# Opening of a two-layer FNet/attention kernel: modulation rows turned by transposes and summed on DVE, held weights' casts, earlier first weights

## Chip, cores and metric

One core of one Trainium2 chip runs the whole program. The metric is the device time of one execution in microseconds; the number given for a kernel is the median of its timed runs. A profile is one more execution, taken by the hardware profiler; its span runs from the first to the last instruction.

## What is computed

Two residual layers on 256 tokens of width 2048, with 256 context tokens beside them (512 columns in all). Layer 0 is a Fourier mixer, layer 1 a windowed attention with a prefix. Every layer first normalises its input and modulates it with a shift, a scale and a gate that a vector `c` gives through a 2048 x 6144 matrix. Cut to the part that the change touches:

```python
for i in range(DEPTH):                      # 2 layers
    shift, scale, gate = split(silu(c) @ ada_w[i] + ada_b[i], 3)
    h = rmsnorm(x, norm_g[i]) * (1 + scale) + shift
    # the same for the context, with c_ctx
    if kind == 0:
        u, z = split(h @ w_in, 2)           # 2048 -> 2 x 4096
        f = real(fft2(u, over tokens and over 256 channels of each of 16 groups))
        y = einsum('bngc,gcd->bngd', f, w_mix) * silu(z)
    ...
    x = x + gate * (y @ w_out[i])
return rmsnorm(x, final_g)
```

## The kernel before

Everything is float32; a product is made as three passes on TensorE (PE): each operand is cast to a rounded half `h` (on ScalarE, ACT) and the difference `l` is made on VectorE (DVE); `split` does this pair and `mm3` the passes h*h, h*l and l*h. The layouts of the weights in memory are prepared so that each load is one tile of 128 partitions by 2048 floats, 1 MB.

The change lies in the opening, which makes three things at once:

- The DFT over tokens of the normalised input. `x_split` splits the input in four blocks `nb` of 512 features, `dft_unit(k)` makes the DFT of one of 16 feature tiles k (128 features each), `evac_dft` copies it out of PSUM, and `scale_hx(k)` later multiplies it by its scale and splits it.
- The modulation rows of layer 0, as 32 strips of the matrix `awp`, 1 MB each. `ada_tile(i)` (L191) loads strip i with `raw_st` and multiplies it with the two modulation vectors (each of the four products counts as two matmuls in the profile, L197). Four strips, two steps, make one bank of PSUM for four feature tiles: scale (`which` = 1) or shift (0). The four products of a strip go to four 32-partition blocks, two rows of each in use, so the bank holds partial sums in four blocks. `ada_rows` (L199) copies the bank to `rows` on ACT (L201). `ada_fin` (L204) turns the rows into columns and sums the four blocks in one go, by four matmuls with `rows` as weights and a 128 x 2 selector `sel` (L207), and adds the bias on DVE (L210, L212) to give `gs0` or `sh0`.
- The first weights: halves kh = 0 and 1 of groups g = 0 and 1 of `wu`, tiles (g, kh). `load_uh` loads one, `fold_uh` (L122) makes a difference `wm` (L124) and a sum (L126) of its two parts on DVE, `split_uh` (L132) splits both into four tiles.

`opening_step(p)` (L269), p from 0 to 15, runs two strips and the work between them; at odd p the row copy follows. Steps over 7 have no DFT unit left and take units of `fill` by `fill_pe` (L372), three matmuls each, from the products of groups 0 and 1 with the 16 scaled tiles: there are 80 units, 56 of them in the steps and 24 behind the last. `fix_f0(nb)` sets column 0 of four scaled tiles from the shift, so a product that reads column 0 (parts `p` and `s`) waits for the shift and one of part `m` doesn't.

Strips and first weights share five slots of 1 MB: three of the pool `raw` (loads at L46) and two of the opening alone (L185). `raw_st` takes the slot whose number `until` is lowest; a strip has its own step there, a first weight the second argument. All these loads are issued by SyncE (SP), whose queue is in order: a load waits until the last reader of its slot is done, and those behind it wait too. Small loads go by ACT's queue, some by GpSimd's (POOL), which also issues a loading sum in later groups (L129).

Behind the opening the loop over 16 groups follows. `load_m(g)` (L323) prepares the mixing matrix, `part` makes the products of a group (parts m and p), `mix` multiplies with the mixing matrix (L463). `asp` (L440, L441 on ACT, L443 on DVE) holds the products of part `s`, and the first `mix` reads it.

Which order the instructions have on each engine is not the order of the text alone: the framework schedules them by its own estimate of when each can start. `tc.issue_after(ins)` binds that: what the block issues on the engine of `ins` comes behind `ins` on it.

Of the kernel before, what the change touches and what calls it, by code (L numbers as in the profile page):

```python
# [28 lines left out]
def tile_dit(ctx: ExitStack, tc: tile.TileContext, a: dict, out: bass.AP):  # L29
# [42 lines left out]
    def mm3(o, wh, wl, xh, xl, start, stop):  # L72
        PE.matmul(o, wh, xh, start=start, stop=False)  # L73
        PE.matmul(o, wh, xl, start=False, stop=False)  # L74
        PE.matmul(o, wl, xh, start=False, stop=stop)  # L75

    def rsqrt(pool, src, w, tag):
        v = pool.tile([P, w], F32, tag=tag + "v", name=tag + "v")
# [37 lines left out]
    sel = const.tile([P, 2], F32, name="sel")  # L116
    V.tensor_reduce(sel, ident.rearrange("p (c s) -> p s c", s=32)[:, 0:2, :], axis=AX.X, op=ALU.add)
# [23 lines left out]
    def load_u(g, after=None):  # L141
        v = [load_uh(g, kh) for kh in range(2)]
        with tc.issue_after(after) if after else nullcontext():
            return [split_uh(*fold_uh(v[kh], g, kh)) for kh in range(2)]

    lay0 = ctx.enter_context(ExitStack())
    adap = lay0.enter_context(tc.tile_pool(name="ada", bufs=1))
# [8 lines left out]
    with tc.tile_pool(name="st", reuse_waits="tile", bufs=1, side="right") as st:  # L156
# [29 lines left out]
            return t  # L186

        oa = [None]
        f0_end = [None]

        def ada_tile(i):  # L191
            nb, which, kg = i // 8, 1 - i // 4 % 2, i % 4
            t = raw_st(a["awp"][which, nb, kg], i // 2)
            if kg == 0:
                oa[0] = psum()
            for j in range(4):
                PE.matmul(oa[0][j * 32 : (j + 1) * 32, :], c32[:, kg * 4 + j, :], t[:, j * 512 : (j + 1) * 512], start=kg == 0, stop=kg == 3)  # L197

        def ada_rows():  # L199
            rows = st.tile([P, 512], F32, tag="rows", name="rows")  # L200
            S.copy(rows, oa[0])  # L201
            return rows

        def ada_fin(nb, which, rows):  # L204
            o2 = psum()
            for j in range(4):
                PE.matmul(o2[:, j * 2 : (j + 1) * 2], rows[:, j * P : (j + 1) * P], sel, start=True, stop=True)  # L207
# [31 lines left out]
        def dft_unit(k, ss_=(0, 1)):  # L239
            nb, j = k // 4, k % 4  # L240
            if k not in od:
                od[k] = psum()
            q = slice(j * P, (j + 1) * P)
            for s in ss_:
                for tt in range(2):
                    t = s * 2 + tt
                    h, l = xs[nb, t]
                    mm3(od[k][:, s * N : (s + 1) * N], h[:, q], l[:, q], dh[:, t, :], dl[:, t, :], tt == 0, tt == 1)

        def evac_dft(k):  # L250
            o = od.pop(k)
            r = act()
            S.copy(r, o)
            V.tensor_copy(f0[:, k, :], o[:, 0::N])
            hx.append(r)
# [10 lines left out]
        raws = {}  # L266
        units = {1: (), 2: (4, 5), 3: (6, 7), 4: (8, 9), 5: (10, 11), 6: (12, 13), 7: (14, 15)}

        def opening_step(p):  # L269
            nb, which = p // 4, 1 - p // 2 % 2  # L270
            if p == 0:
                x_split(0)
                for k in range(4):
                    dft_unit(k, (0,))
            for i in (2 * p, 2 * p + 1):
                ada_tile(i)
            if p in uload:
                raws[uload[p]] = load_uh(*uload[p], raw_st, {0: 7, 1: 12}[uload[p][1]])
            if p % 2:
                rows = ada_rows()  # L280
            if p == 1:
                for k in range(4):
                    dft_unit(k, (1,))
                    if k == 1:
                        ada_fin(nb, which, rows)
                for k in range(4):
                    evac_dft(k)
            else:
                for n, k in enumerate(units.get(p, ())):
                    dft_unit(k)  # L290
                    evac_dft(k)
                    if n == 0 and p % 2:
                        ada_fin(nb, which, rows)
                if p > 7:
                    fill_pe(4)
                    if p % 2:
                        ada_fin(nb, which, rows)
                    fill_pe(3)
# [52 lines left out]
        def u_step(g, nm, k):  # L351
            c0, c1 = dict(m=(128, 256), p=(0, 130))[nm]
            if k == 0:
                ou[g][nm] = psum()[0:127, 0 : 2 * (c1 - c0)].rearrange("p (s j) -> p s j", s=2)
            wh, wl = wu[g][k // 8][nm]
            h, l = hx[k]
            mm3(ou[g][nm], wh[:, k % 8, :], wl[:, k % 8, :], h[:, :, c0:c1], l[:, :, c0:c1], k == 0, k == KT - 1)

        def sp_step(k):
            if k == 0:  # L360
                ou[0]["s"] = psum()[0:32, 0:260].rearrange("p (s j) -> p s j", s=2)
            h, l = hx[k]
            q = slice(k * 32, (k + 1) * 32)
            mm3(ou[0]["s"], sph[:, q], spl[:, q], h[:, :, 0:130], l[:, :, 0:130], k == 0, k == KT - 1)
# [7 lines left out]
        def fill_pe(n):  # L372
            for _ in range(n):
                g, nm, k = fill.pop(0)
                sp_step(k) if nm == "s" else u_step(g, nm, k)

        for p in range(8, 16):
            if p == 8:
                wu[1][0] = split_uh(*raws[1, 0])
# [25 lines left out]
    ft_end = [None, None]  # L405
    asp = up.tile([96, 2, 130], F32R, name="asp", bufs=1)
    for g in range(G):
        w = load_u(g, f0_end[0] if g == 2 else None) if g > 1 else wu[g]
        if g == 0:
            am = []  # L410
            for i in range(2):
# [26 lines left out]
        if g == 0:  # L438
            ov = ou[0]["s"]
            S.copy(asp[0:32], ov)  # L440
            S.copy(asp[64:96], ov)  # L441
            pqh, pql, sp = m0
            V.tensor_tensor(asp[32:64], ov, asp[0:32].bitcast(F32), op=ALU.subtract)  # L443
# [726 lines left out]
```

## Time and profile before

| | us |
|---|---|
| median of 3 runs | 1876.44 (1874.44 to 1877.57) |
| the profiled execution | 1873.82 |
| its span | 1871.9 |
| PE busy in the span | 1826.4 (98%) |
| DVE busy | 1388.7 (74%) |
| ACT busy | 953.9 (51%) |
| mean granted clock of PE | 0.992 |

The profile's page gives busy time by engine, a picture of the span in 40 slices, the DMA queues, the chain of work that ended last, and the costliest groups of instructions. In the chain PE has 88% of the span. Other views of the same trace give the instructions of one engine in order of time, with the idle time before each and what ended it, and the busy time of every engine in a stretch. Times in them count from the span's start. The opening lasts to about 136 us; the strips' matmuls run from 17.37 to 120 us, and the eight row copies from 26.88 to 120.67 us.

### The profile page before, as it was taken

To read this page: it belongs to the slowest core of one execution; us is meant where nothing else is said; L and a number is where in the kernel's file an instruction comes from. 1 tells how busy PE (TensorE), PEld (TensorE's weight loads), DVE (VectorE), ACT (ScalarE), POOL (GpSimd) and SP (SyncE) were. 2 spreads that over 40 slices of the span, in tenths; PEclk is the share of its full clock that TensorE was granted. 3 is DMA by queue.
4 is the path that set the end of the run, shared out by engine and by line. 5 is a ranking of instruction groups with operands and counts; after the bars stand their busy time and mean duration, and the time that the engine had idled before them with its cause. 6 is when DMAs were issued, how large, how long until landed. Compare 5 with 4: busy or idle time off the path is not lost.

```text
span 1871.9 us, 26517 instructions
## 1 busy us (share of the span) xinstructions
PE 1826.4 (98%) x9921; PEld 1556.5 (83%) x9921; DVE 1388.7 (74%) x2760; ACT 953.9 (51%) x1661; POOL 175.3 (9%) x188
## 2 busy tenths in 40 slices
PE   6889999999999999999999999999999999999997
PEld 4669999888888888888888787888888888887886
DVE  4558888787768788687984835788778878887455
ACT  4435444432222243224221524888888888896343
POOL 0002111200000000000000001102221220300001
PEclk9999999999999999999999999999999999999999
DMA  9988888756666647763576323333333333434553
GB/s 395 352 299 235 227 224 233 253 219 230 236 230 222 228 163 259 281 224 135 224 268 224 131 90 135 136 128 120 125 124 135 116 132 134 159 135 171 189 180 135
DMA packets 75089, 366.89 MB, mean 196 GB/s; under 512 B 22161, under 2 KB 22305, under 8 KB 39889
## 3 DMA queue, kind: packets, MB, share of 16 engines
q1 hardware_dynamic: 49104, 324.83, 47.5%
q0 software_dynamic: 21280, 32.63, 6.8%
q10 hardware_dynamic: 4576, 7.74, 1.3%
q8 instruction: 78, 1.28, 0.3%
q14 instruction: 51, 0.41, 0.1%
HBM read 352.58 MB, written 12.59 MB: 195 GB/s over the span
## 4 chain that ended last, share of the span: by engine, by line
PE 88%; DVE 4%; DMA 3%; issue 2%; ACT 2%; POOL 0%; SPq 0%; POOLq 0%; ACTq 0%; DVEq 0%
PE ps L73 22%; PE ps L74 22%; PE ps L75 22%; PE ps L869 6%; PE ps L871 3%; PE ps L925 3%; DMA raw<-in_wu 2%; PE ps L940 2%; PE ps L939 2%; PE ps L905 1%; PE ps L906 1%; PE ps L197 1%; DMA raw<-in_awp 1%; DVE wpl L61 1%; ACT wh L60 0%
## 5 line engine op out<-in xcount | busy, mean ns | idle before, releaser
L60 ACT CAST wh<-raw 128x1024 fp32r<-128x1024 f32 x333 | 349.4, 1051 | 560.4 <-PE ps L74 496.1
L61 DVE TENSOR_TENSOR wl<-raw,wh 128x1024 fp32r<-128x1024 f32 x333 | 421.2, 1267 | 262.7 <-ACT wh L60 259.8
L74 PE MATMUL ps<-act,wh 128*128 128x512 f32 x1024 | 398.3, 389 | 0.0
L73 PE MATMUL ps<-act,wh 128*128 128x512 f32 x1024 | 393.7, 389 | 0.0
L75 PE MATMUL ps<-act,wl 128*128 128x512 f32 x1024 | 391.3, 389 | 0.0
L75 PEld LDWEIGHTS ps<-act,wl 128*128 128x128 f32 x1024 | 192.2, 188 | 39.9
L74 PEld LDWEIGHTS ps<-act,wh 128*128 128x128 f32 x1024 | 192.2, 188 | 39.8
L73 PEld LDWEIGHTS ps<-act,wh 128*128 128x128 f32 x1024 | 192.2, 188 | 39.8
L869 PE MATMUL ps<-h,wh 128*128 128x512 f32 x512 | 187.0, 400 | 0.0
L504 DVE CUSTOM_DVE_ANT_0 raw<-raw,cb 128x512 f32<-128x512 f32 x256 | 172.4, 687 | 18.8 <-DMA raw<-in_adw 15.0
L871 PE MATMUL ps<-h,wl 128*128 128x256 f32 x512 | 138.2, 280 | 0.0
L504 DVE CUSTOM_DVE_ANT_0 junk<-raw,cb 128x512 f32<-128x512 f32 x192 | 131.6, 685 | 6.7 <-ACT cb L496 5.6
L74 PE MATMUL ps<-wl,h 128*128 128x512 f32 x320 | 125.8, 393 | 1.5 <-DVE wl L61 1.5
L73 PE MATMUL ps<-wh,h 128*128 128x512 f32 x320 | 124.5, 397 | 0.2 <-ACT h L688 0.2
L75 PE MATMUL ps<-wh,h 128*128 128x512 f32 x320 | 124.5, 391 | 0.0
L869 PEld LDWEIGHTS ps<-h,wh 128*128 128x128 f32 x512 | 96.2, 188 | 19.0
L907 DVE CUSTOM_DVE_ANT_0 ps<-ps,mask,nsink 128x512 f32<-128x512 f32 x128 | 92.1, 753 | 12.3 <-PE ps L906 11.4
L910 ACT ACTIVATE p<-ps,mx 128x512 f32<-128x512 f32 x128 | 87.2, 686 | 24.7 <-DVE mx L907 24.1
L871 PEld LDWEIGHTS ps<-h,wl 128*128 128x128 f32 x512 | 96.8, 189 | 1.4
L61 DVE TENSOR_TENSOR pl<-ps,ph 128x512 fp32r<-128x512 f32 x128 | 83.6, 684 | 10.0 <-ACT ph L60 8.8
L915 ACT ACTIVATE p<-p,sm 128x512 f32<-128x512 f32 x128 | 85.5, 717 | 7.8 <-DVE sm L913 7.8
L74 PE MATMUL ps<-wl,ys 128*128 128x512 f32 x212 | 83.3, 393 | 0.0
(307 smaller groups left out, 3579.7 us busy)
## 6 DMA issues: line engine op xcount, KB each, us to landing
raw<-in_wz SPq DMA_DIRECT2D x64, 1024.0 KB, 4.9
raw<-in_adw SPq DMA_DIRECT2D x64, 1024.0 KB, 4.9
raw<-in_awp SPq DMA_DIRECT2D x32, 1024.0 KB, 8.6
raw<-in_wo SPq DMA_DIRECT2D x32, 1024.0 KB, 5.6
raw<-in_wq SPq DMA_DIRECT2D x32, 1024.0 KB, 4.8
raw<-in_wu SPq DMA_DIRECT2D x32, 1016.0 KB, 7.2
raw<-in_wo1b SPq DMA_DIRECT2D x16, 1024.0 KB, 4.8
act<-in_xT POOLq DMA_DIRECT2D x32, 256.0 KB, 5.2
```

Of the source, the lines that this page charges most:

```text
L60: S.copy(h, src)
L61: V.tensor_tensor(l, src, h.bitcast(F32), op=ALU.subtract)
L73: PE.matmul(o, wh, xh, start=start, stop=False)
L74: PE.matmul(o, wh, xl, start=False, stop=False)
L75: PE.matmul(o, wl, xh, start=False, stop=stop)
L504: V.tensor_tensor_reduce(junk if s == 0 and i < 3 else wf, wf, cb[:, s, kq * 512 : kq * 512 + 512], 1.0, 0.0, ALU.mult, ALU.add, acc[:, i, ...
L869: PE.matmul(o[0], wh[:, q], hx1[k], start=k == 0, stop=k == KT - 1)
L871: PE.matmul(o[0][:, 0:N], wl[:, q], hx1[k][:, 0:N], start=False, stop=False)
L907: V.tensor_tensor_reduce(o, o, mask[:, tb, :], -0.125, nsink[:, i : i + 1], ALU.add, ALU.min, mx[:, tb : tb + 1])
L910: S.activation(pt[:, tb, :], so[tb], AF.Exp, bias=mx[:, tb : tb + 1], scale=-1.0, accum_out=sm[:, tb : tb + 1])
L915: S.activation(pt[:, tb, :], pt[:, tb, :], AF.Copy, scale=sm[:, tb : tb + 1])
L925: PE.transpose(o[:, (kt * 2 + tb) * P : (kt * 2 + tb + 1) * P], pt[:, tb, c : c + P], ident)
```

## The change

- `ada_fin` is given an instruction `behind`. It makes four transposes of `rows` (128 x 128 each, a whole bank) instead of four matmuls with `sel`, puts them behind that instruction on PE, and sums the four blocks on DVE with one reduction of 128 x 32 elements to 128 x 8. `sel` and its reduction are gone.
- The turn of a step's rows is kept in `pend` and made after the first strip of the next step, with that strip's last matmul as `behind`; the last one comes after four units of the fill.
- In a step the first DFT unit, or three units of the fill, now stand ahead of the two strips, the rest behind them.
- The first weights (0, 0) and (1, 0) are loaded at steps 4 and 5 instead of 5 and 6; their `until` is 6 and 7 instead of 7, that of (0, 1) 11 instead of 12.
- The splits of all four first weights are issued behind the latest row copy at that place: those of steps 5, 7, 11 and 13.
- In group 2 the second half's fold and split, and `load_m(2)`, are issued behind the last instruction of `asp`. For groups over 2 both halves are loaded and folded before the first is split.

```diff
-        def ada_fin(nb, which, rows):
+        def ada_fin(nb, which, rows, behind):
             o2 = psum()
-            for j in range(4):
-                PE.matmul(o2[:, j * 2 : (j + 1) * 2], rows[:, j * P : (j + 1) * P], sel, start=True, stop=True)
+            with tc.issue_after(behind):
+                for j in range(4):
+                    PE.transpose(o2[:, j * P : (j + 1) * P], rows[:, j * P : (j + 1) * P], ident)
             kq = slice(nb * 4, nb * 4 + 4)
             dst = (sh0, gs0)[which][:, kq, :]
-            V.tensor_tensor(dst, o2[:, 0:8].rearrange("p (a b) -> p a b", b=2), adab[:, 0, which, kq], op=ALU.add)
+            V.tensor_reduce(dst, o2.rearrange("p (a j s) -> p a s j", a=4, j=4)[:, :, 0:2, :], axis=AX.X, op=ALU.add)
+            V.tensor_tensor(dst, dst, adab[:, 0, which, kq], op=ALU.add)
...
+            us_ = units.get(p, ())
+            if us_:
+                dft_unit(us_[0])
+                evac_dft(us_[0])
+            elif p > 7:
+                fill_pe(3)
             for i in (2 * p, 2 * p + 1):
-                ada_tile(i)
+                r = ada_tile(i)
+                if pend:
+                    ada_fin(*pend.pop(), r)
             if p in uload:
-                raws[uload[p]] = load_uh(*uload[p], raw_st, {0: 7, 1: 12}[uload[p][1]])
+                raws[uload[p]] = load_uh(*uload[p], raw_st, uhold[uload[p]])
             if p % 2:
-                rows = ada_rows()
+                pend.append((nb, which, ada_rows()))
...
-        uload = {5: (0, 0), 6: (1, 0), 9: (0, 1), 10: (1, 1)}
+        uload = {4: (0, 0), 5: (1, 0), 9: (0, 1), 10: (1, 1)}
+        uhold = {(0, 0): 6, (1, 0): 7, (0, 1): 11, (1, 1): 12}
...
-        opening_step(6)
         wu = [[None, None], [None, None]]
         raws[0, 0] = fold_uh(raws[0, 0], 0, 0)
+        opening_step(6)
+        with tc.issue_after(rows_end[0]):
+            wu[0][0] = split_uh(*raws[0, 0])
+        raws[1, 0] = fold_uh(raws[1, 0], 1, 0)
         opening_step(7)
-        wu[0][0] = split_uh(*raws[0, 0])
-        raws[1, 0] = fold_uh(raws[1, 0], 1, 0)
+        with tc.issue_after(rows_end[0]):
+            wu[1][0] = split_uh(*raws[1, 0])
...
                 if p == q + 1:
-                    wu[kh][1] = split_uh(*raws[kh, 1])
+                    with tc.issue_after(rows_end[0]):
+                        wu[kh][1] = split_uh(*raws[kh, 1])
+        while fill[0][2] < 12:
+            fill_pe(1)
+        r = fill_pe(4)
+        ada_fin(*pend.pop(), r)
         fix_f0(3)
         fill_pe(len(fill))
...
+        if g == 2:
+            v = [load_uh(g, kh) for kh in range(2)]
+            w = []
+            for kh in range(2):
+                with tc.issue_after((f0_end[0], asp_end)[kh]):
+                    w.append(split_uh(*fold_uh(v[kh], g, kh)))
...
-            with tc.issue_after(f0_end[0]) if g == 1 else nullcontext():
+            with tc.issue_after((f0_end[0], asp_end)[g - 1]) if g < 3 else nullcontext():
                 pqh, pql, sp = load_m(g)
```

More of the change, by code (lines that the diff above doesn't have):

```diff
@@ L74, in mm3 @@
         PE.matmul(o, wh, xl, start=False, stop=False)
-        PE.matmul(o, wl, xh, start=False, stop=stop)
+        return PE.matmul(o, wl, xh, start=False, stop=stop).ins
     def rsqrt(pool, src, w, tag):
@@ L115, in tile_dit @@
     V.tensor_copy(c32[:, :, 0:2], cc)
-    sel = const.tile([P, 2], F32, name="sel")
-    V.tensor_reduce(sel, ident.rearrange("p (c s) -> p s c", s=32)[:, 0:2, :], axis=AX.X, op=ALU.add)
     def load_uh(g, kh, ld=raw, *until):
@@ L139, in split_uh, with load_u @@
         return fl
[L141 to L144, printed above, removed]
+    def load_u(g):
+        return [split_uh(*f) for f in [fold_uh(load_uh(g, kh), g, kh) for kh in range(2)]]
     lay0 = ctx.enter_context(ExitStack())
@@ L188, in tile_dit @@
         oa = [None]
+        rows_end = [None]
         f0_end = [None]
@@ L196, in ada_tile @@
             for j in range(4):
-                PE.matmul(oa[0][j * 32 : (j + 1) * 32, :], c32[:, kg * 4 + j, :], t[:, j * 512 : (j + 1) * 512], start=kg == 0, stop=kg == 3)
+                r = PE.matmul(oa[0][j * 32 : (j + 1) * 32, :], c32[:, kg * 4 + j, :], t[:, j * 512 : (j + 1) * 512], start=kg == 0, stop=kg == 3)
+            return r.ins
         def ada_rows():
             rows = st.tile([P, 512], F32, tag="rows", name="rows")
-            S.copy(rows, oa[0])
+            rows_end[0] = S.copy(rows, oa[0]).ins
             return rows
-        def ada_fin(nb, which, rows):
+        def ada_fin(nb, which, rows, behind):
             o2 = psum()
-            for j in range(4):
-                PE.matmul(o2[:, j * 2 : (j + 1) * 2], rows[:, j * P : (j + 1) * P], sel, start=True, stop=True)
+            with tc.issue_after(behind):
+                for j in range(4):
+                    PE.transpose(o2[:, j * P : (j + 1) * P], rows[:, j * P : (j + 1) * P], ident)
             kq = slice(nb * 4, nb * 4 + 4)
             dst = (sh0, gs0)[which][:, kq, :]
-            V.tensor_tensor(dst, o2[:, 0:8].rearrange("p (a b) -> p a b", b=2), adab[:, 0, which, kq], op=ALU.add)
+            V.tensor_reduce(dst, o2.rearrange("p (a j s) -> p a s j", a=4, j=4)[:, :, 0:2, :], axis=AX.X, op=ALU.add)
+            V.tensor_tensor(dst, dst, adab[:, 0, which, kq], op=ALU.add)
             if which:
@@ L247, in dft_unit @@
                     h, l = xs[nb, t]
-                    mm3(od[k][:, s * N : (s + 1) * N], h[:, q], l[:, q], dh[:, t, :], dl[:, t, :], tt == 0, tt == 1)
+                    r = mm3(od[k][:, s * N : (s + 1) * N], h[:, q], l[:, q], dh[:, t, :], dl[:, t, :], tt == 0, tt == 1)
+            return r
         def evac_dft(k):
@@ L264, in scale_hx @@
             hx[k] = (h.rearrange("p (s j) -> p s j", s=2), l.rearrange("p (s j) -> p s j", s=2))
-        raws = {}
+        raws, pend = {}, []
         units = {1: (), 2: (4, 5), 3: (6, 7), 4: (8, 9), 5: (10, 11), 6: (12, 13), 7: (14, 15)}
@@ L283, in opening_step @@
                     dft_unit(k, (1,))
-                    if k == 1:
-                        ada_fin(nb, which, rows)
                 for k in range(4):
                     evac_dft(k)
[L288 to L298, printed above, removed]
+            elif us_:
+                dft_unit(us_[1])
+                evac_dft(us_[1])
+            elif p > 7:
+                fill_pe(4)
             if p in (1, 3, 5):
@@ L356, in u_step @@
             h, l = hx[k]
-            mm3(ou[g][nm], wh[:, k % 8, :], wl[:, k % 8, :], h[:, :, c0:c1], l[:, :, c0:c1], k == 0, k == KT - 1)
+            return mm3(ou[g][nm], wh[:, k % 8, :], wl[:, k % 8, :], h[:, :, c0:c1], l[:, :, c0:c1], k == 0, k == KT - 1)
         def sp_step(k):
@@ L363, in sp_step @@
             q = slice(k * 32, (k + 1) * 32)
-            mm3(ou[0]["s"], sph[:, q], spl[:, q], h[:, :, 0:130], l[:, :, 0:130], k == 0, k == KT - 1)
+            return mm3(ou[0]["s"], sph[:, q], spl[:, q], h[:, :, 0:130], l[:, :, 0:130], k == 0, k == KT - 1)
         fill = [(g, nm, k) for g in range(2) for nm in ("m", "p") for k in range(8)]
@@ L374, in fill_pe @@
                 g, nm, k = fill.pop(0)
-                sp_step(k) if nm == "s" else u_step(g, nm, k)
+                r = sp_step(k) if nm == "s" else u_step(g, nm, k)
+            return r
         for p in range(8, 16):
             if p == 8:
-                wu[1][0] = split_uh(*raws[1, 0])
                 cst = ua.tile([P, 4, P], F32, name="cst", bufs=1)
@@ L407, in tile_dit @@
     for g in range(G):
-        w = load_u(g, f0_end[0] if g == 2 else None) if g > 1 else wu[g]
+        if g == 2:
[4 more added lines that the diff above has]
+                    w.append(split_uh(*fold_uh(v[kh], g, kh)))
+        else:
+            w = load_u(g) if g > 1 else wu[g]
         if g == 0:
@@ L442, in tile_dit @@
             pqh, pql, sp = m0
-            V.tensor_tensor(asp[32:64], ov, asp[0:32].bitcast(F32), op=ALU.subtract)
+            asp_end = V.tensor_tensor(asp[32:64], ov, asp[0:32].bitcast(F32), op=ALU.subtract).ins
         mh, ml = am[g % 2]
```

## The prediction

> **What bounds the kernel now.** I read the table of busy shares first: PE 1826.4 us of a span of 1871.9, so all that can be had without removing PE work is 45 us. Then the table of stretches, to see where they lie.
>
> ```profile
> 30.00:40.00 10.00, 10.00 (x67) 5.50 (x60) 2.77 (x8) 4.06 (x10) 0.00 (x0) 0.85 1.01 414
> 60.00:70.00 10.00, 6.63 (x45) 4.99 (x45) 9.36 (x25) 7.18 (x15) 0.00 (x0) 0.85 1.02 425
> 70.00:80.00 10.00, 10.00 (x67) 7.13 (x65) 3.01 (x11) 1.21 (x2) 0.00 (x0) 0.81 0.88 325
> 80.00:90.00 10.00, 8.72 (x69) 4.87 (x68) 5.19 (x9) 5.31 (x10) 0.00 (x0) 1.00 0.83 323
> 130.00:140.00 10.00, 7.17 (x39) 6.95 (x38) 9.84 (x13) 3.59 (x6) 0.00 (x0) 0.66 0.81 181
> 150.00:160.00 10.00, 10.00 (x87) 10.00 (x85) 9.17 (x14) 5.27 (x10) 2.58 (x3) 1.00 0.89 283
> ```
>
> Columns: stretch, length, busy PE, PEld, DVE, ACT, POOL, granted clock, DMA share, GB/s. From 150 us PE makes 87 matmuls in 10 us, one per 0.115 us: its full rate, and it keeps it to 343 us but for some 2.7 us of gaps. So a microsecond won before 140 us should reach the end. Up to 60 us the transfers are full (413 to 424 GB/s, a 1 MB strip tile each 2.5 us; 352 in the last ten). From 50 to 120 us the stretches show 352, 425, 325, 323, 368, 416, 355 GB/s; against 420 they lack 376 x 10 us / 420 = 9.0 us. That is the most by which the last strip can come sooner. The third view is PE's timeline, first around 66 us, then at the end of the opening.
>
> ```profile
> 66.87 1.71 PE L207 MATMUL ps<-sel,rows 128*128 128x2 f32 x8 [3.37 <-ACT rows L201]
> 71.28 1.94 PE L197 MATMUL ps<-raw,c 128*32 128x512 f32 x8
> 76.77 1.06 PE L197 MATMUL ps<-raw,c 128*32 128x512 f32 x8
> ```
>
> ```profile
> 112.05 1.07 PE L197 MATMUL ps<-raw,c 128*32 128x512 f32 x8
> ...
> 113.87 1.05 PE L207 MATMUL ps<-sel,rows 128*128 128x2 f32 x8 [0.52 <-ACT rows L201]
> 114.86 2.78 PE L197 MATMUL ps<-raw,c 128*32 128x512 f32 x24
> ...
> 123.53 0.39 PE L73 MATMUL ps<-act,wph 128*127 128x260 f32 x1 [0.86 <-DVE act L221]
> ...
> 133.05 0.58 PE L463 MATMUL ps<-asp,sp 96*128 96x260 f32 x1 [2.83 <-DVE asp L443]
> ```
>
> In brackets stands PE's idle time and who ended it. L207 is the old turn of the modulation rows; it waits for the row copy L201. After the 3.37 us the same strip (8 matmuls, L197) takes 1.94 instead of 1.06 us: PE restarts at half rate, and the clock column shows 0.81. ACT's timeline says why that copy was late:
>
> ```profile
> 63.23 1.02 ACT L60 CAST wph<-raw 128x1016 fp32r<-128x1016 f32 x1
> 64.17 1.70 ACT L262 ACTIVATE act<-act,gs 128x256 fp32r<-128x256 f32 x4
> 65.77 0.56 ACT L253 COPY act<-ps 128x512 f32<-128x512 f32 x1
> 66.23 0.58 ACT L201 COPY rows<-ps 128x512 f32<-128x512 f32 x1
> ```
>
> Strip 15 ended at 63.5 us; the copy started at 66.23, behind a weights' cast and scalings.
>
> **Turn and sum (gain).** Before strip 15 the transfers set the pace, so I count nothing there. Behind it, PE waits for row copies 3.37 + 0.76 + 0.76 + 0.52 us (at 66.87, 83.69, 100.39, 113.87) and 0.86 at 123.53 for what follows the last: 6.3 us. With the turn behind the next strip (1.0 us of PE against 0.83 us from strip end to copied row) these go, if that strip has landed; if not, the turn and, behind it on PE, the second strip and the fill wait with it. The half rate after 66.87 goes with its wait: turn 1.57 us where 0.95 is usual, twelve matmuls 2.84 for 1.45, strip 1.86 for 1.00: 2.9 us. A turn of eight passes takes 0.91 to 0.98 us; the nearest row to four transposes is this one, 0.11 us each, so 0.44 us:
>
> ```profile
> 1041.59 2.78 PE L633 MATMUL ps<-ident,act 128*128 128x128 f32 x24
> ```
>
> Five turns by 0.5 us: 2.5. Together A = 11.7 us; bounds 9.0 (the transfers' slack) and 11.7. [...] DVE gains a reduction of 128x32 to 128x8 from PSUM, which no row shows: between 0.16 (a 128x8 reduction) and 0.69 (a 128x512 pass from PSUM), I take 0.2, the near row; eight of them, 1.6 us, lie in DVE's idle time (100 to 110 us: 1.16 busy of 10); without that cover only the last counts, 0.2. The removed sum into sel (0.17) was hidden.
>
> **Order behind asp (gain).** The last source of the wait at 133.05 is DVE's order:
>
> ```profile
> 128.87 0.42 DVE L329 TENSOR_TENSOR mt<-m 128x256 f32<-128x256 f32 x1
> 129.21 0.42 DVE L330 TENSOR_TENSOR mt<-m 128x256 f32<-128x256 f32 x1
> ...
> 132.57 0.42 DVE L443 TENSOR_TENSOR asp<-ps,asp 32x260 fp32r<-32x260 f32 x1
> ```
>
> asp's ACT inputs end at 128.36. The change puts group 2's second fold (1.17) and its load_m sums (0.67) behind it: 1.8 of the 2.83 us surely go. The remaining 1 us is of the size after which the rows show no slow phase (0.76, 0.86), so also the half rate goes: from 133.43, 12 matmuls at 0.215 and 18 in 3.35 us against 0.12 each, 2.3 us. B = 4.1; bounds 1.8 (half rate stays) and 5.1. What is pushed back, that fold's sums, is wanted some 5.8 us after asp (first mix 1.7, load_m 1.2, eight k of the first part 2.9) and needs about 3.5 (fold, cast, difference), so nothing for it.
>
> **Held casts (loss).** The edge puts each cast behind a row copy in ACT's order, so what ACT has queued behind the cast (scalings, evacuations) and DVE behind its difference waits for a strip too; ACT is busy only 3 to 7 of 10 there, so I price the slot: a first-weights tile keeps its slot of the five until its last difference. By the slot rule strip 28 takes the slot of the tile (1,1), whose casts now stand behind the row copy of step 13, that is behind strip 27. Before, its cast ran at 95.81, 17 us ahead of that copy. From strip 27's end: row copied 0.83, two casts 1.88 (63.23 to 64.17 is one), difference 1.21, the load at its shortest 4.8 (the shortest strip load in the trace is 4.7): 8.7 us, where it was 1.8. Behind strip 28 wait the scale rows of the last four k and all they feed; strips 29 to 31 have other slots. PE can fill with steps 14 and 15, 14 units of 0.36 us: 5.1. Idle 3.6, and a restart like that at 66.87, 2.9: C = 6.5; bounds 0 (more fill is left for it) and 11.6 (none). [...]
>
> **First weights sooner (loss).** The tile (0,0) was landed at 45.6 and not folded before 54.91, since x's strips hold the buffers; loading it a step sooner wins nothing and keeps a slot longer. On SP each of the two loads passes two strips: 10 to 13 land one transfer (2.5 us) later, 14 as before, and PE has the DFT units for that. Strip 15 now takes that slot, freed at 61.3 by the old times, where it was issued at 56.4; strip 18 takes (1,0)'s, held behind strip 15's row copy. SP's queue is in order, but strips 16 and 17 have free slots and can be ordered ahead. D between 0 and 4.9; I take 2.
>
> **The rest.** For groups over 2 both folds now come before both splits. Their data come some 4.5 us apart, and a split also waits for its buffers; I take 0, with -2.7 (the loop's gaps go) and +14.7 (13 groups by one fold of 1.13 us ahead of a split that PE awaits) as ends. Handing back instructions costs nothing.
>
> **Sum:** 11.7 + 4.1 - 6.5 - 2 = 7.3 us less. The profiled run took 1873.8 us with a span of 1871.9, so a span of about 1864.6; against the median of the runs shown, 1876.44 (2.6 over the profiled one), 1869.1.
>
> **Rivals.** (1) The holds starve the strips, and it is slower: C at its upper end 11.6, D at 4.9, and strip 27 behind tile (0,1): 8.7 less three transfers of 2.5 leaves 1.2, with a restart of 2.9, 4.1. 20.6 - 15.8 = +4.8, 1881. For it: with two weights held only three slots stream, and the median strip load is 8.6 us. Against: the fill. It decides where the last row copy, at 120.08 now, comes after some 124.2, where B no longer pays for it. (2) The gain stops at DVE: it has hardly a gap from 123.89 to 150, so PE can be ahead of it only by the slack at group 2. If strip 28 holds the last shift rows, DVE's block starts about 2 us sooner and the end moves by as little: 1874. For it: 9.84 of 10 busy; against: part of that block is what is pushed behind asp. (3) The holds cost nothing: 9.0 + 5.1 = 14.1, 1862. For it: the fill has 24 units more; against: eight of these need strip 27's rows, whose turn now stands behind strip 28. (4) The folds' order costs the loop half its upper end, 7.4 us, and the gain is gone: 1876. For it: PE waited for apl at 261.4 and 277.0 already.
>
> **Chances.** Forecast 0.42 (own range 1865 to 1873), rival 1 0.24, rival 2 0.14, rival 3 0.16, rival 4 0.04. A measurement here tells about 0.2%, 3.8 us, from no change. Faster: forecast and rival 3, 0.58. Same: rivals 2 and 4, 0.18. Slower: 0.24. The range takes in rival 3's value and rival 1's: 1861 to 1882.
>
> **What would show it.** A: no idle before the transposes, about 0.11 us each, and no clock of 0.81 around 70 us. B: the gap before L463 at most 1 us and a clock near 1 there. C: a gap before strip 28, its load issued right after a difference of the held tile. D: strip 15's row copy not later than about 68 us. Wrong if the last row copy comes after 120, or if the loop from group 2 shows gaps that it did not have.

## The result and the profile after

| | before | after |
|---|---|---|
| median, us (20 runs each, on the same chip) | 1875.74 | 1872.45 |
| lowest and highest run | 1872.73, 1882.31 | 1868.70, 1877.71 |
| the profiled execution | 1873.82 | 1872.59 |
| its span | 1871.9 | 1869.5 |
| PE busy in the span | 1826.4 | 1822.9 |
| DVE busy | 1388.7 | 1390.0 |
| mean granted clock | 0.992 | 0.991 |
| first product with `asp` starts at | 133.05 | 130.80 |

The ratio is 0.9981 with an interval of 0.9973 to 0.9990: 3.6 us less (1.9 to 5.1). The kernel became faster, by half of the 7.3 us that were forecast. Single executions of one kernel are up to 10 us apart, so a difference of 2 or 3 us between two profiled spans is no evidence; below, totals are read from medians, and the profiles only for what stands where.

The same stretches of the kernel after, in the columns of the prediction's first view (stretch, length, busy PE, PEld, DVE, ACT, POOL, granted clock, DMA share, GB/s):

```profile
60.00:70.00 10.00, 6.06 (x45) 2.82 (x43) 5.20 (x14) 5.50 (x13) 0.00 (x0) 0.96 1.02 418
70.00:80.00 10.00, 8.85 (x52) 5.11 (x52) 7.75 (x21) 3.22 (x5) 0.00 (x0) 0.70 1.00 377
80.00:90.00 10.00, 10.00 (x79) 7.08 (x78) 2.82 (x11) 2.75 (x7) 0.00 (x0) 1.00 0.93 350
90.00:100.00 10.00, 6.05 (x38) 1.64 (x38) 6.26 (x9) 3.60 (x6) 0.00 (x0) 0.83 0.96 365
...
130.00:140.00 10.00, 8.05 (x53) 7.61 (x52) 9.88 (x17) 3.82 (x10) 2.11 (x2) 0.83 0.70 138
```

PE is still busy only 6 of 10 us from 60 to 70, and now from 90 to 100 too, where it was at 9.63. The clock near 70 us, 0.81 before, is 0.70. From 50 to 120 us the transfers make 319, 418, 377, 350, 365, 394, 301 GB/s, which lacks 9.9 us at 420, where it lacked 9.0. PE's timeline says what it waits for:

```profile
67.95 1.06 PE L194 MATMUL ps<-raw,c 128*32 128x512 f32 x8 [2.96 <-DMA raw<-in_awp]
71.15 1.94 PE L194 MATMUL ps<-raw,c 128*32 128x512 f32 x8 [2.13 <-DMA raw<-in_awp]
73.02 1.12 PE L206 MATMUL ps<-ident,rows 128*128 128x128 f32 x4
...
91.65 1.06 PE L194 MATMUL ps<-raw,c 128*32 128x512 f32 x8 [0.56 <-DMA raw<-in_awp]
94.31 1.06 PE L194 MATMUL ps<-raw,c 128*32 128x512 f32 x8 [1.59 <-DMA raw<-in_awp]
97.17 1.94 PE L194 MATMUL ps<-raw,c 128*32 128x512 f32 x8 [1.80 <-DMA raw<-in_awp]
```

No transpose (L206) waits any more: the five waits for row copies, 6.2 us together from 35 to 136 us, are gone. In their place stand five waits for strips (L194), 9.0 us together, where there was none. The half rate came along (granted clock 0.50 from 69.24 to 76.07): the strip at 71.15 takes 1.94 us, the turn behind it 1.04.

The end of the opening, from the same view of the kernel after:

```profile
113.48 0.66 PE L206 MATMUL ps<-ident,rows 128*128 128x128 f32 x4
113.89 0.37 PE L73 MATMUL ps<-act,wmh 128*127 128x256 f32 x1
...
124.09 0.39 PE L73 MATMUL ps<-act,wph 128*127 128x260 f32 x1 [1.09 <-DVE act L221]
...
130.80 0.39 PE L480 MATMUL ps<-asp,sp 96*128 96x260 f32 x1 [0.51 <-DVE asp L460]
...
133.82 0.38 PE L73 MATMUL ps<-mh,ch 128*128 128x256 f32 x1 [1.44 <-ACT mh L60]
...
134.19 0.42 PE L73 MATMUL ps<-act,wmh 128*127 128x256 f32 x1
134.41 0.42 PE L74 MATMUL ps<-act,wmh 128*127 128x256 f32 x1
```

Four transposes take 0.41 us, from 113.48 to the start of the next product. The wait of 2.83 us for `asp` is one of 0.51. A new wait of 1.44 us follows, for group 2's mixing matrix, and behind it products start 0.21 us apart, the half rate (granted clock 0.50 from 134.09 to 137.51).

When each strip landed, and when PE began to multiply it (us), worked out from SP's queue and PE's timeline. Strips are numbered in the order in which PE takes them, and each is paired with its own load by the semaphore that PE waits for, since SP issues some loads in another order. "No holds" is the kernel e3 below, one of its executions.

| strip | before: landed, multiplied | after | no holds |
|---|---|---|---|
| 13 | 50.74, 56.13 | 57.95, 61.01 | 57.40, 60.56 |
| 16 | 64.49, 71.28 | 71.01, 71.15 | 70.98, 71.11 |
| 22 | 90.78, 91.97 | 91.60, 91.65 | 89.05, 93.06 |
| 24 | 94.67, 101.37 | 97.03, 97.17 | 94.00, 96.42 |
| 31 | 115.97, 118.95 | 117.97, 120.57 | 114.40, 116.31 |

Before, a strip lay in its slot for 1 to 7 us until PE came to it; PE was the late one. After, strips 16, 22 and 24 are multiplied within 0.14 us of landing: PE came earlier, the strips didn't. The last one landed 2.0 us later than before. For the waits at 67.95 and 71.15 (5.1 us), SP's order counts too: after the change the load of strip 17 was issued at 54.77, ahead of those of strips 15 and 16 (57.99 and 62.14); it landed at 64.06 and lay unused until 74.06, while PE waited for the other two. No run tries another order there.

### The profile page after: what moved, and what is told of

Its sections match the earlier page's. It is cut to its first block, busy times and chain, and to the rows that moved or that the text cites. A ratio compares the mean times of both kernels' runs of the same rounds, so it can differ in the third digit from the quotient of the medians.

```text
span 1869.5 us, 26460 instructions
## 1 busy us (share of the span) xinstructions
PE 1822.9 (98%) x9889; PEld 1550.9 (83%) x9889; DVE 1390.0 (74%) x2767; ACT 954.8 (51%) x1661; POOL 175.3 (9%) x188
## 4 chain that ended last, share of the span: by engine, by line
PE 86%; DMA 5%; DVE 4%; issue 2%; ACT 2%; POOL 0%; SPq 0%; ACTq 0%; POOLq 0%; DVEq 0%
PE ps L73 22%; PE ps L74 22%; PE ps L75 22%; PE ps L886 6%; DMA raw<-in_wu 3%; PE ps L888 3%; PE ps L942 3%; PE ps L957 2%; PE ps L956 2%; PE ps L922 1%; PE ps L923 1%; PE ps L194 1%; DMA raw<-in_awp 1%; DVE wpl L61 1%; DVE wm L122 0%
## 5 line engine op out<-in xcount | busy, mean ns | idle before, releaser
L75 PE MATMUL ps<-wh,h 128*128 128x512 f32 x320 | 124.2, 391 | 0.0
```

What stands on the lines that cost most here:

```text
L75: return PE.matmul(o, wl, xh, start=False, stop=stop).ins
```

## The experiments

Medians and ratios, each against the kernel before on the same chip, with the gain worked out from the ratio. The two last columns come from one profiled execution each (us): the start of the first product with `asp` (133.05 before), and the time for which the four first weights hold their slots, from the issue of the load to the end of the difference `wpl`, the last to read the slot, summed over the four (86.8 before).

| kernel | median (before) | ratio | gain, us | asp at | slots held |
|---|---|---|---|---|---|
| the change | 1872.45 (1875.74) | 0.9981 [0.9973, 0.9990] | 3.6 | 130.80 | 114.4 |
| e1 | 1871.50 (1876.13) | 0.9976 [0.9966, 0.9985] | 4.5 | 130.76 | 86.8 |
| e2 | 1877.85 (1876.13) | 1.0007 [0.9998, 1.0017] | -1.3 | 133.29 | 114.5 |
| e3 | 1866.82 (1876.13) | 0.9958 [0.9945, 0.9970] | 7.9 | 126.53 | 66.3 |
| e4 | 1872.32 (1876.13) | 0.9986 [0.9973, 1.0000] | 2.6 | 132.34 | 115.4 |
| g1 | 1870.80 (1874.70) | 0.9981 [0.9973, 0.9990] | 3.6 | 125.64 | 83.4 |
| g2 | 1870.23 (1874.70) | 0.9980 [0.9969, 0.9991] | 3.7 | 129.85 | 96.5 |
| g3 | 1870.90 (1874.70) | 0.9982 [0.9971, 0.9993] | 3.4 | 128.33 | 63.8 |
| g4 | 1870.41 (1874.70) | 0.9983 [0.9971, 0.9996] | 3.2 | 128.41 | 82.3 |
| h1 | 1872.85 (1875.69) | 0.9989 [0.9978, 1.0000] | 2.1 | 133.18 | 116.6 |
| h2 | 1870.30 (1875.69) | 0.9973 [0.9962, 0.9984] | 5.1 | 129.86 | 110.1 |
| h3 | 1867.58 (1875.69) | 0.9962 [0.9947, 0.9976] | 7.1 | 128.92 | 66.9 |
| h4 (e3 again) | 1869.11 (1875.69) | 0.9967 [0.9956, 0.9978] | 6.2 | 129.35 | 67.2 |

### e1 and e2: the order behind asp alone, and all but it

e1 is the kernel before with these lines alone; e2 is the changed kernel without them.

```diff
+        if g == 2:
+            v = [load_uh(g, kh) for kh in range(2)]
+            w = []
+            for kh in range(2):
+                with tc.issue_after((f0_end[0], asp_end)[kh]):
+                    w.append(split_uh(*fold_uh(v[kh], g, kh)))
...
-            with tc.issue_after(f0_end[0]) if g == 1 else nullcontext():
+            with tc.issue_after((f0_end[0], asp_end)[g - 1]) if g < 3 else nullcontext():
```

> The kernel before with the last part of the change alone: group 2's second fold and its load_m behind asp. Theory 1 (all of the measured gain comes from this part, and the opening gives back what it wins): the opening up to the last row copy is as before (120.1 us), the idle time before the first product with asp falls from 2.83 to about 0.5 us, a wait for load_m's cast of some 1.4 us appears behind it, and the span is about 1869.5, 2 to 3 us under before. Theory 2 (the opening's part wins by itself, and this one hardly): the span is within 1 us of 1871.9.

> The changed kernel without that last part. Theory 1: the waits for strips at 68, 71 and 91 to 97 us stay, the last row copy is at about 121.7 us, the wait for asp of some 2.8 us is back, and the span is within 1 us of 1871.9. Theory 2: the span is 1869 to 1870.5.

e1 gains 4.5 us (2.8 to 6.4), e2 nothing that can be told (1.3 slower, from 0.4 faster to 3.2 slower; its profiled span, 1874.8, is above both expected values). The two kernels agree: with holds, the whole gain of the change is the order behind `asp`, and the rest of the edit wins nothing that can be told. e1's timeline of PE, and of DVE before it:

```profile
130.76 0.39 PE L470 MATMUL ps<-asp,sp 96*128 96x260 f32 x1 [0.51 <-DVE asp L450]
...
133.79 0.39 PE L73 MATMUL ps<-mh,ch 128*128 128x256 f32 x1 [1.44 <-ACT mh L60]
...
134.13 0.28 PE L73 MATMUL ps<-act,wmh 128*127 128x256 f32 x1
134.25 0.28 PE L74 MATMUL ps<-act,wmh 128*127 128x256 f32 x1
```

```profile
130.29 0.42 DVE L450 TENSOR_TENSOR asp<-ps,asp 32x260 fp32r<-32x260 f32 x1
130.74 1.22 DVE L124 TENSOR_TENSOR wm<-raw 128x1016 f32<-128x1016 f32 x1
131.87 0.42 DVE L329 TENSOR_TENSOR mt<-m 128x256 f32<-128x256 f32 x1
132.21 0.42 DVE L330 TENSOR_TENSOR mt<-m 128x256 f32<-128x256 f32 x1
```

e1 reaches `asp` at 130.76, the changed kernel at 130.80: in these two executions all that the new opening moved came to nothing by that point. (One kernel's executions can be 2.8 us apart there, as e3 and h4 show; the evidence is e2's median.) Behind `asp` come the fold (`wm`) and then the two sums `mt`, whose cast to `mh` the product at 133.79 waits for: 1.44 us that were not there before. The first 30 products from `asp` on take 5.38 us, this wait among them, where they took 6.20 before at half rate (granted clock 0.50 from 131.92 to 138.75). By the trace the order wins 2.3 us up to `asp` and 0.8 behind it, 3.1, inside the interval of the medians.

### e3, h4 and e4: no holds, and later loads

e3 and h4 are one kernel: the changed one without the edge around the splits of the four first weights.

```diff
-        with tc.issue_after(rows_end[0]):
-            wu[0][0] = split_uh(*raws[0, 0])
+        wu[0][0] = split_uh(*raws[0, 0])
...
-        with tc.issue_after(rows_end[0]):
-            wu[1][0] = split_uh(*raws[1, 0])
+        wu[1][0] = split_uh(*raws[1, 0])
...
-                    with tc.issue_after(rows_end[0]):
-                        wu[kh][1] = split_uh(*raws[kh, 1])
+                    wu[kh][1] = split_uh(*raws[kh, 1])
```

e4 keeps the holds and puts the first two loads back to steps 5 and 6.

```diff
-        uload = {4: (0, 0), 5: (1, 0), 9: (0, 1), 10: (1, 1)}
-        uhold = {(0, 0): 6, (1, 0): 7, (0, 1): 11, (1, 1): 12}
+        uload = {5: (0, 0), 6: (1, 0), 9: (0, 1), 10: (1, 1)}
+        uhold = {(0, 0): 7, (1, 0): 7, (0, 1): 12, (1, 1): 12}
```

> The changed kernel with the casts of the four first weights free in their order. Theory 1a (the held casts keep their slots and so starve the strips: 114 us of slot time in the changed kernel, 87 before): the weights' differences end sooner, the strips' waits at 91 to 97 us (about 4 us) go, the last row copy comes 2 to 5 us sooner and the span is 1865 to 1867.5. Theory 1b (the strips' transfers are late because two loads of weights stand ahead of them, not because of the holds): nothing changes within 1 us. Theory 3 (the row copies need the holds): the row copies of steps 7 and 11 come behind two casts again, PE waits there, and the span is 1870 to 1873.

> The changed kernel with the first weights loaded at steps 5 and 6 and their slot numbers as before. Theory 1a: the waits for strips at 68 and 71 us (5.1 us) shrink to half since the slots are free for strips 14 to 17, but those at 91 to 97 us stay: span 1867 to 1869. Theory 1b: both shrink, span 1864 to 1867. Theory 4 (sooner loads are what makes the first weights ready in time): waits for weights appear near 60 us, span 1870 to 1873.

> The kernel without holds once more, since its five runs are few and executions of one kernel here spread by some 10 us: if its gain is real, 6 to 9 us under before again and the first product with asp at 126 to 127 us; if the five runs were lucky, 3 to 5 us. The trace also shows how far the same kernel's loop over groups differs from one execution to the next (211.0 us from the first asp product to the next stage in the run before).

Without holds the kernel gains 7.9 us (5.6 to 10.3) in e3 and 6.2 (4.1 to 8.3) in h4, against 3.6 with them: by these gains the holds cost 2.6 to 4.3 us. The interval of e3 lies clear of the changed kernel's (1.9 to 5.1), that of h4 overlaps it; a third kernel without holds, h3 below, gains 7.1. The waits at 91 to 97 us are gone, as theory 1a had it. e3 and h4 are one kernel and yet reach `asp` at 126.53 and 129.35, where 126 to 127 was expected: in h4 the half rate near 30 us lasts 6.8 us against 3.4 in e3, and its second row copy comes at 42.92 against 41.15. ACT's timeline of the changed kernel shows the hold of the last two weights:

```profile
95.49 0.59 ACT L199 COPY rows<-ps 128x512 f32<-128x512 f32 x1 [4.35 <-PE ps L194]
95.97 1.04 ACT L60 CAST wmh<-wm 128x1016 fp32r<-128x1016 f32 x1
...
109.34 0.59 ACT L199 COPY rows<-ps 128x512 f32<-128x512 f32 x1 [11.38 <-PE ps L194]
109.82 1.04 ACT L60 CAST wmh<-wm 128x1016 fp32r<-128x1016 f32 x1
```

ACT stands idle for 4.35 and 11.38 us with the casts queued behind the copy, and the cast of the sum that lies in the slot (`wph`) comes behind that, at 96.92 and 110.77; in e3 the casts `wmh` of these two ran at 77.9 and 91.5. Until that second cast and its difference are done the weights' slots take no strip. The stretches of e3 from 70 to 90 us:

```profile
70.00:80.00 10.00, 8.89 (x59) 5.11 (x60) 5.35 (x16) 1.66 (x3) 0.00 (x0) 0.83 1.01 419
80.00:90.00 10.00, 10.00 (x81) 7.15 (x80) 5.89 (x15) 5.25 (x12) 0.00 (x0) 1.00 1.01 413
```

The transfers make 419 and 413 GB/s where the changed kernel has 377 and 350. But PE still waits for strips, by the view of its waits in e3 from 35 to 136 us (total, times, longest):

```profile
PE ps L194 <- DMA raw<-in_awp: 6.3, 3, 4.7
```

6.3 us is as much as the row copies had cost before (6.2). The longest, 4.7 us, is for strip 16, which landed at 70.98: its load was issued at 61.69, behind that of strip 17 and right behind strip 13's last matmul (61.62), so it waited for a strip's slot and not for a weight's. So holds or none, moving the turn exchanged one wait for another of its size.

e4 measures as the changed kernel does. (Its profiled span, 1866.6, lies where theory 1b had it, but that execution was the fastest of its nine.) Its trace shows that the sooner loads have a price at their place: with loads at steps 5 and 6, strip 13 lands at 50.64 and strip 16 at 64.15, with sooner ones at 57.95 and 71.01, and the transfers make 400 GB/s from 50 to 60 us against 319. The end doesn't show it. In e4 the weights hold their slots elsewhere, (0, 1) for 40.8 us against 34.8, and PE waits 9.5 us for strips; that this is the reason isn't shown.

### g1, g2, g3: which holds, and which loads

g1 keeps the holds on (0, 0) and (1, 0) alone, g2 those on (0, 1) and (1, 1) alone; g3 has none and e4's later loads. Each is a part of the diffs above:

```diff
 # g1
-                    with tc.issue_after(rows_end[0]):
-                        wu[kh][1] = split_uh(*raws[kh, 1])
+                    wu[kh][1] = split_uh(*raws[kh, 1])
 # g2
-        with tc.issue_after(rows_end[0]):
-            wu[0][0] = split_uh(*raws[0, 0])
+        wu[0][0] = split_uh(*raws[0, 0])
...
-        with tc.issue_after(rows_end[0]):
-            wu[1][0] = split_uh(*raws[1, 0])
+        wu[1][0] = split_uh(*raws[1, 0])
 # g3: no hold, and
+        uload = {5: (0, 0), 6: (1, 0), 9: (0, 1), 10: (1, 1)}
+        uhold = {(0, 0): 7, (1, 0): 7, (0, 1): 12, (1, 1): 12}
```

> The changed kernel with the holds on the casts of (0,0) and (1,0) alone. If slot time is what counts, these two holds cost 15.7 us of it (47.5 against 31.8 without holds), a third of what all four cost: waits for strips near 68 us return, none at 91 to 97, span 1865.5 to 1867. If the first holds are the dear ones (the waits at 68 and 71 us set everything behind them), the span is 1868 to 1870.

> The changed kernel with the holds on the casts of (0,1) and (1,1) alone. By slot time (67 us held against 34.5 without) these are the dear ones: the waits for strips at 91 to 97 us and a last strip loaded behind the difference of (1,1) return, last row copy 119.5 to 121.5, span 1867 to 1869. If they cost nothing, the span is within 1 us of 1864.7.

> No holds, and the first weights loaded at steps 5 and 6 as before. If the sooner load takes slots from the strips (theory 1a), the wait of 4.7 us for a strip at 71 us shrinks and the span is 1861 to 1864. If the sooner load is what the first fill needs, or if the scheduler moves the loads anyway, it is 1864 to 1868.

By the medians the two pairs can't be told apart (3.6 and 3.7 us). The profiles hint that the second pair is the costly one: with it PE reaches `asp` at 129.85 and waits 7.8 us for strips, with the first pair at 125.64 and 6.2. The waits went as expected: g2 has those between 91 and 97 us again (1.16 at 93.17, 1.91 at 96.15), and g1, like e3, h3 and h4, has none there; so these waits come with the second pair's holds. But e3 and h4, one kernel, are already 2.8 us apart at `asp`, so the price of each pair isn't shown. The gap between 125.64 and 129.85 did not come out at the end either, for the loop over groups took 208.3 us in g2 and 214.4 in g1, from the first product with `asp` to the start of the next stage, the products for `z`. That length differs between executions of every kernel here, 206.6 to 214.4 (210.9 before, 210.7 after), and takes part of what the opening wins. Most of the difference between g1 and g2 can be read: in the loop PE stands idle for 6.2 us in g1 and 2.2 in g2, and g1 has a half-rate phase of 3.4 us (at 185.32), of which the clock of 0.50 costs an estimated half: 5.7 us together of 6.1. Why the idle time differs no run isolates.

g3 has full transfers over a longer stretch:

```profile
80.00:90.00 10.00, 7.39 (x62) 4.32 (x54) 5.86 (x11) 4.31 (x8) 0.00 (x0) 1.00 1.02 423
90.00:100.00 10.00, 8.79 (x57) 5.69 (x58) 4.12 (x19) 2.15 (x5) 0.00 (x0) 0.83 1.01 419
```

The wait of 4.7 us is short there (0.17 at 71.24, 1.42 at 73.72). Yet the profiled span, 1869.0, lies above both expected ranges, and the gain is 3.4 us, less than e3's and h4's. So without holds the sooner loads help by some 3 us rather than harm, though the intervals of g3 and h4 overlap. That also bounds the price of the holds: it is shown for sooner loads (2.6 to 4.3); with later ones, g3 against e4, it is 0.8, inside the noise.

### g4: the transposes in the old place

The kernel before with e1's lines and the turn by transposes and a reduction, neither moved nor held.

```diff
-                PE.matmul(o2[:, j * 2 : (j + 1) * 2], rows[:, j * P : (j + 1) * P], sel, start=True, stop=True)
+                PE.transpose(o2[:, j * P : (j + 1) * P], rows[:, j * P : (j + 1) * P], ident)
...
-            V.tensor_tensor(dst, o2[:, 0:8].rearrange("p (a b) -> p a b", b=2), adab[:, 0, which, kq], op=ALU.add)
+            V.tensor_reduce(dst, o2.rearrange("p (a j s) -> p a s j", a=4, j=4)[:, :, 0:2, :], axis=AX.X, op=ALU.add)
+            V.tensor_tensor(dst, dst, adab[:, 0, which, kq], op=ALU.add)
```

> The kernel before with the order behind asp and the turn by transposes in its old place, nothing else of the opening. If the turn's passes count on PE where it is the bound (five turns by 0.5 us), the span is 1.5 to 3 us under that of the run with the order alone (1869.1), so 1866 to 1867.6, and PE still waits for each row copy. If the strips' transfers are the bound there, the span is 1868.5 to 1870.

From the third row copy to `asp` g4 takes 76.7 us and e1 79.0: 2.3 sooner, near the 2.5 that five cheaper turns were priced at. The waits for row copies stay, 6.3 us. The median doesn't show the 2.3 (3.2 us of gain against e1's 4.5, with intervals of some 2 us to either side), and the same stretch differs by 1.0 us between e3 and h4 (73.1 and 74.1), so the 2.3 is likely but not shown to reach the end.

g3 is g4 with the turn moved behind the next strip and the units around it in the new order (besides these, the first weights are folded earlier, and later groups fold both halves first). The two measure alike, 3.4 and 3.2 us of gain, and reach `asp` at 128.33 and 128.41. In g4 PE waits 6.3 us for row copies and never for a strip; in g3 it waits 7.7 for strips and 1.5 for row copies. That is the most direct evidence that moving the turn by itself wins nothing here, to within the 2 us or so that these intervals can tell.

### h1, h2, h3: what of a hold costs, and load_m

h1 holds only the cast of the difference `wm`, which doesn't read the slot; h2 only the cast of the sum, which does. h3 has no holds and `load_m(2)` not behind `asp`.

```diff
 # h1 with nm == "m", h2 with nm == "p"; the splits are given rows_end[0] as hold
-            split(h, l, t)
+            with tc.issue_after(hold) if hold and nm == "m" else nullcontext():
+                split(h, l, t)
 # h3, besides the three holds
-            with tc.issue_after((f0_end[0], asp_end)[g - 1]) if g < 3 else nullcontext():
+            with tc.issue_after(f0_end[0]) if g == 1 else nullcontext():
```

> The changed kernel with the holds on the casts of the differences wm alone, which lie in a buffer of their own; the casts that read the load's slot are free. If the holds cost by the slots that they keep, this is like no holds: the four tiles keep their slots for 65 to 80 us in all, the first product with asp comes at 125.5 to 128 us, and the median is 6 to 9 us under before. If they cost by making the weights late for the fill, it is like the changed kernel: first product with asp at 129.5 to 131, 3 to 4 us under before.

> The other half of that: the holds on the casts that read the load's slot alone, those of wm free. By slots: 105 to 115 us of slot time, the first product with asp at 129.5 to 131 us, 3 to 4 us under before. By late weights: half the cost at most, 127 to 129 us.

> No holds, and load_m(2) not put behind asp; group 2's second fold still is. If the wait of 1.44 us behind the first mix is the price of that hold, it goes, with the slow clock behind it (about 1.5 us), while the wait for asp grows by at most the two sums, 0.7 us: the loop's second mix comes 1.5 to 2.5 us sooner after the first product with asp than in the run without holds. If DVE is the bound there, it comes no sooner.

h1 was to free the slots and keep the casts late, and didn't: ACT's order left the slot's cast behind the held one, so its slots are held 116.6 us and it gains 2.1, below both of the ranges expected. In its ACT timeline a row copy starts at 96.84, the held cast of `wm` at 97.32, the free cast at 98.26.

h2 reaches `asp` at 129.86 with slots held 110.1, as was expected if the slots cost the time; its gain of 5.1, though, lies above that case's 3 to 4. In it too the free casts came late, behind the held ones (the cast of `wm` at 96.39, behind the held one at 95.44). So whether the late slots or the late casts cost the time stays open: no kernel here has one without the other. h3's wait of 1.44 us for `mh` stays, at 131.95, and its gain, 7.1 us, is that of e3 and h4: on DVE the fold still goes ahead of the sums `mt`. That the edge on `load_m` makes this wait is refuted; that the fold makes it is read from the order alone.

## Why the prediction was half right

**Direction and order behind asp: right.** B was 4.1; alone it measures 4.5 (2.8 to 6.4), and it is the whole gain. The wait fell from 2.83 to 0.51 us, "at most 1" as told, and in e1 the half rate behind it went (granted clock 1.00 from 120 to 136 us, where it was 0.87 before; in the changed kernel the half rate came 3.3 us later, at 134.09). That what is pushed back costs nothing was wrong: the prediction counted the fold's own sums, wanted 5.8 us behind `asp`; `mh` from `load_m(2)` is wanted 1.6 us behind it (133.79 less 1.44 less 130.76), and PE waits 1.44.

**Turn and sum: the prices right, the worth wrong.** Four transposes take 0.41 us (0.44 foretold), the reduction 0.19 (0.2), and no turn waits. The step that failed is A's size: 11.7, with the 9.0 us that the transfers lacked as its lower bound. With holds, A less C and D, 3.2 by the forecast, measures -1.3 (-3.2 to 0.4) in e2, and `asp` is reached at 130.76 in e1 and 130.80 after; without holds, e3 and h4 less e1 leave 1.7 to 3.4 us, where A - D was 9.7. The error was to count the transfers' slack as time that an earlier PE would win back. The table of strips shows that before the change strips waited for PE, by 6.8 us at strip 16. PE could come sooner by about that much before it met the landing times. Those hang on slots, which the weights hold for 86.8 us already before the change and for 114.4 after it, and the transfers' lack went from 9.0 to 9.9 us. g3 against g4 shows the same without holds: 3.4 and 3.2 us of gain with the turn moved and in its place. The clause "if that strip has landed" stood in the prediction without a price. It was the price: 9.0 us of waits for strips against 6.2 for rows.

**Held casts: a loss as told, size and place off.** C was 6.5; the holds cost 2.6 to 4.3 us. A slot freed by a held tile's difference does come late, but it went to another strip: tile (1, 1)'s difference ended at 113.24 (112.03 + 1.21 in DVE's timeline), the next strip load was issued at 113.27, and it was strip 31's, not 28's. Strip 28 was multiplied at 112.49 without a wait. The waits for strips stand earlier, from 91.65 to 97.17. The loads of those three strips were issued at 85.22, 86.64 and 91.15, each right behind the end of an earlier strip on PE (85.15, 86.58, 91.09), while the weights held two slots (from 64.62 to 99.39 and from 81.14 to 113.24); in e3 the first of these slots took a strip at 82.84, right behind the difference's end at 82.81. Whether the late slots or the late casts make up the cost stays open (h1 and h2). At the last strip PE's fill covered the lateness.

**First weights sooner: seen at its place, not at the end.** Strips 13 and 16 land 7.3 and 6.9 us later than with the old steps (e4), more than the 2.5 of one transfer. The end doesn't confirm a loss of 2: e4 equals the change, and without holds sooner loads look better by some 3.

**The sum by what was measured:** without holds, the opening's part 1.7 to 3.4 and B 4.5 make 6.2 to 7.9; less the holds' 2.6 to 4.3, 3.6. Against the forecast, A less D was too high by 6.3 to 8.0 us and C by 2.2 to 3.9. The two errors have opposite signs in the sum, so that the median, 1872.45, still lies in the forecast's own range (1865 to 1873) is partly luck.

**The rivals.** The starving of strips (1) happened, 9.0 us of waits, but it cost about what the turn had saved and little more (e2, -1.3); the last row copy came at 121.70, short of the 124.2 from which it was to decide. By its own mark, "wrong if the last row copy comes after 120", the forecast of the opening was wrong: that copy came 1.6 us later than before. `asp` came 2.25 sooner all the same, by DVE's order. The stop at DVE (2) is not what bounded it: the strips' waits stand ahead of it, and without the holds PE reached `asp` at 126.53 and 129.35 with the same wait for DVE there, 0.51. That holds cost nothing (3) fell, for the sooner loads at least. The folds' order in the loop (4) wasn't tried alone; the loop's length after is that of before, 210.7 against 210.9.

**A version that beats both.** The change without holds, timed twice, gains 6.2 and 7.9 us on the kernel before, where the change gains 3.6.

## What to carry to other kernels

Before a wait is priced as a gain, put beside it when the next supplier is ready: here each strip's landing time, which showed how far PE could come forward before it would wait for something else. An edge that protects one queue's order also stretches the life of every buffer that the held instruction reads; add up the buffers' held time before and after (86.8 and 114.4 us here, 66 without the edges). When a change has several parts, run each alone: one of them, a few lines of DVE's order, had the whole gain that was measured.

## What was not expected of the hardware

The same idle gap was followed by two different speeds. Ahead of the product with `mh` PE stood still for 1.44 us in e1 and in the changed kernel, after the same instructions; e1 went on at a product each 0.12 us, with a granted clock of 1.00 from 120 to 136 us, the changed kernel at 0.21, with a clock of 0.50 from 134.09 to 137.51. In the changed kernel a gap of 1.09 us at 124.09 was followed by full rate (the clock was 1.00 from 99.96 to 134.09), one of 1.80 at 97.17 by a strip of 1.94 us; in the kernel before, one of 1.11 at 29.71 was followed by a strip of 1.94 us too. So in these traces the length of the gap alone doesn't say whether the clock drops.

The granted clock tells where it dropped. In the traces of the kernel before and of the changed one, up to 350 us, the stretches with a clock of 0.50 last 3.41 or 6.83 us, and within one execution they start whole multiples of 3.413 us apart: before at 29.52, 67.07 and 131.92 (11 and 19 of them), after at 31.69, 69.24, 96.55 and 134.09 (11, 8 and 11). Why they do isn't shown. In the changed kernel the 3.41 us ahead of 134.09 hold the whole gap of 1.44 us, and PE was busy for 1.85 of them. The gap of 1.80 us that ended at 97.17 came one strip after a gap of 1.59; in the 3.41 us from 93.14 PE was busy 1.06 us, and the clock halved at 96.55, before the second gap had ended. Busy time is not a clean rule either: before the change PE was busy 1.78 of the 3.41 us from 15.87, less than 1.85, and the clock was 1.00 up to 29.52. What made e1 go on at full rate and the changed kernel at half, behind the same gap, is not shown.
